# Row maxima of 16,384 rows on one core: the first load as two transfers from two queues

## The chip, the cores and the metric

The kernel runs on one core of one Trainium2 chip. The metric is the device time of one execution in microseconds (us). Lower is better.

## The reference

The input `x` has 32 x 512 rows of 1,024 float32 values, 67.11 MB in all. The output is the maximum of each row, 16,384 float32 values.

```python
def reference(x: np.ndarray) -> np.ndarray:
    return np.max(x, axis=-1).astype(np.float32)
```

## The kernel before

The 16,384 rows are dealt out to the 128 partitions of the on-chip memory, so that a partition has 128 rows (called columns of the result here). They are split into two blocks of 112 and 16 columns. Within a block, partition p holds neighbouring rows of `x`, and a load fetches n rows for each of the 128 partitions, 4 KB a row and partition. The list `BLOCKS` gives the n of each load: 2, 15, 16, 14, 11, 11, 10, 10, 8, 8, 7 for the first block and 3, 3, 3, 2, 1, 1, 1 for the second. The last two rows of each partition come as four pieces (`PIECES`), each a part of a row.

The loads go into a ring of 47 row slots in one tile named `ring`. The first four loads (2 + 15 + 16 + 14 = 47 rows) fill it exactly. Later loads reuse slots, so each must wait until the rows that lay there have been read and their transfers have landed. The function `issue()` puts each load in program order as early as the ring's list of readers lets it; all loads (line 238) and all pieces (line 243) are issued from the SP queue, one `dma_start` each. In the program's order the four loads that fill the ring stand ahead of every other step.

The work on the rows is written out by hand in `PLAN`. A step `d3` reduces all of load 3 on VectorE (DVE in the profile) with one `reduce_max`; line 78 is the helper that records every such reduction, through `in_turn`, which keeps the order of one engine's instructions. Steps `t`, `b`, `p` and `m` belong to four late loads (10, 13, 14 and 17) that are shared with other engines: TensorE transposes a part of the rows (line 160), ScalarE (ACT) copies the result out (line 166), GpSimd (POOL) reduces over the partitions (line 168), TensorE turns the maxima back (line 178), and VectorE merges. The steps `f0` to `f3` reduce the four pieces at the end. Two stores from the Activation queue (lines 265 and 267) bring the result out.

ScalarE has no work until the first copy for load 10. Its first instruction is a load of its activation table, which the compiler adds and the profile puts down to line 166.

Of the kernel before, what the change touches and what calls it, by code (L numbers as in the profile page):

```python
# [40 lines left out]
def kernel(  # L41
# [5 lines left out]
    nc = tc.nc  # L47
    P = 128
# [22 lines left out]
    def in_turn(engine, inst):  # L71
        if engine in latest:
            tc.add_manual_dep(inst.ins, latest[engine].ins.name, NOSYNC, reason="in turn")
        latest[engine] = inst
        return inst

    def maximum(out, in_):
# [8 lines left out]
        out=colno, data0=ident, data1=ident, initial=-1.0, op0=ALU.add, op1=ALU.mult))  # L86
    in_turn("DVE", nc.vector.transpose(out=rowno, in_=colno[:, :32]))  # L87
    for q in range(1, P // 32):
        part = rowno[q * 32:(q + 1) * 32, 0:1]
        in_turn("DVE", nc.vector.tensor_scalar(  # L90
            out=part, in0=part, scalar1=float(q * 32), scalar2=None, op0=ALU.add))
    identity = in_turn("DVE", nc.vector.tensor_scalar(  # L92
        out=ident, in0=colno, scalar1=rowno[:, 0:1], scalar2=None, op0=ALU.is_equal))
# [41 lines left out]
    def rows(j):  # L135
        start, n, _, _ = loads[j]
        return ring[:, I + start * D:I + (start + n) * D].rearrange("p (i d) -> p i d", d=D)
# [90 lines left out]
    issued = 0  # L228
    behind = None

    def issue():
        nonlocal issued
        while issued < len(loads):
            start, n, src, _ = loads[issued]
            if any(readers[j] and s < start + n and start < s + k
                   for j, (s, k, _, _) in enumerate(loads[:issued])):
                return
            load = nc.sync.dma_start(out=rows(issued), in_=src)  # L238
            issued += 1
        if any(readers[j] and s < at + last + 1 and at < s + k for j, (s, k, _, _) in enumerate(loads)):  # L240
            return
        while pieces:
            nc.sync.dma_start(out=pieces[0][0], in_=pieces[0][1])
            pieces.pop(0)

    for step in PLAN:
        issue()
        kind, k = step[0], int(step[1:])
        if kind in "dp":
            (direct if kind == "d" else partial)(k)  # L250
            readers[k] -= 1
        elif kind == "t":
            turn(k)
            readers[chunks[k][0]] -= 1
        elif kind == "b":
            back(k)
        elif kind == "m":
            merge(k)
        else:
            inst = maximum(*tail[k])  # L260
            if behind is None:
                behind = inst
# [34 lines left out]
```

## Time and profile before

| What | Value |
|---|---|
| time, median of 3 runs | 163.85 us (163.83 to 164.08) |
| span of the profiled execution, first to last instruction | 162.1 us |
| what the median has over that span | 1.75 us (the page gives no other time for the profiled execution) |
| VectorE busy | 135.3 us, 83% of the span |
| TensorE, ScalarE, GpSimd busy | 13.6, 6.3 and 15.9 us |
| bytes read | 67.11 MB, 414 GB/s over the span |
| queue of the loads (q1, issued from SP) | 3,168 packets, 96.8% of what 16 DMA engines can be busy in the span |
| queue of the stores (q10, issued from Activation) | 288 packets, 0.2% |

Times in the profile are counted from the first instruction. An engine's busy time leaves out the instructions that issue transfers, wait or branch. In the timeline a line gives the start, the duration, the engine, the line of the kernel, the operation with its tiles, and in brackets how long the engine was idle before it and what ended the idle time. Merged instructions have one line with their count. "SPq" is the SP engine's own instructions, here the issues of the loads.

### The profile page before, as it was taken

How to read it: one execution, taken by the hardware profiler on the slowest of the kernel's cores; microseconds unless marked ns; L12 is line 12 of the kernel's file. 1: busy time of each engine (PE TensorE's matmuls, PEld its weight loads, DVE VectorE, ACT ScalarE, POOL GpSimd, SP SyncE). 2: the span in 40 equal slices, each digit the busy share in tenths (PEclk: the TensorE clock that was granted, in tenths of full speed). 3: DMA queues.
4: the chain of work that ended last, by engine and by line, in shares of the span. 5: the costliest groups of instructions: out<-in, count | busy, mean ns of one | idle time of the engine just before them, and what ended most of it. 6: DMA issues, size and time to landing. Idle time of an engine off the chain costs nothing.

```text
span 162.1 us, 295 instructions
## 1 busy us (share of the span) xinstructions
PE 13.6 (8%) x76; PEld 11.7 (7%) x76; DVE 135.3 (83%) x33; ACT 6.3 (4%) x7; POOL 15.9 (10%) x10
## 2 busy tenths in 40 slices
PE   0000000000000000000000000000000000772942
PEld 0000000000000000000000000000000000762731
DVE  3500019998399999999999999996999999999994
ACT  3000000000000000000000000000000000241120
POOL 0000000000000000000000000000000000099791
PEclk9999999999999999999999999999999999996555
DMA  5995999599879999898999799799999989999991
GB/s 178 566 485 258 470 501 517 259 517 517 354 340 439 453 404 534 356 523 367 478 411 475 334 485 475 334 485 388 477 429 388 466 382 446 415 421 416 411 388 34
DMA packets 3456, 67.18 MB, mean 414 GB/s; under 512 B 640, under 2 KB 896, under 8 KB 1536
## 3 DMA queue, kind: packets, MB, share of 16 engines
q1 hardware_dynamic: 3168, 67.11, 96.8%
q10 hardware_dynamic: 288, 0.07, 0.2%
HBM read 67.11 MB, written 0.07 MB: 414 GB/s over the span
## 4 chain that ended last, share of the span: by engine, by line
DMA 50%; DVE 47%; SPq 1%; issue 0%; DVEq 0%
DMA ring<-in_x_dram 50%; DVE ring L78 45%; DVE joint L78 2%; SPq L238 1%; DVEq L292 0%
## 5 line engine op out<-in xcount | busy, mean ns | idle before, releaser
L78 DVE TENSOR_REDUCE ring<-ring 128x1 f32<-128x1024 f32 (+13 forms) x20 | 129.9, 6547 | 23.5 <-DMA ring<-in_x_dram 23.5
L168 POOL PARTITION_ALL_REDUCE top<-sb x6 | 15.7, 2658 | 142.6 <-ACT sb L166 142.5
L160 PE MATMUL ps<-ident,ring 128*128 128x128 f32 x38 | 9.0, 423 | 140.0 <-DMA ring<-in_x_dram 140.0
L160 PEld LDWEIGHTS ps<-ident,ring 128*128 128x128 f32 x38 | 7.6, 225 | 140.1 <-issue 140.1
L166 ACT COPY sb<-ps 128x1024 f32<-128x1024 f32 (+2 forms) x6 | 5.0, 834 | 150.5 <-PE ps L160 143.5
L78 DVE TENSOR_REDUCE joint<-ring 128x2 f32<-128x1280 f32 (+1 forms) x3 | 3.9, 1314 | 0.0
L178 PE MATMUL got<-ident,top 1*128 1x1 f32 x24 | 2.7, 228 | 3.8 <-POOL top L168 3.6
L178 PEld LDWEIGHTS got<-ident,top 1*128 1x128 f32 x24 | 2.4, 188 | 4.6 <-POOL top L168 4.6
L178 PE MATMUL joint<-ident,top 1*128 1x1 f32 x14 | 2.0, 244 | 1.9 <-POOL top L168 1.9
L178 PEld LDWEIGHTS joint<-ident,top 1*128 1x128 f32 x14 | 1.7, 210 | 2.7 <-POOL top L168 2.7
L166 ACT ACT_TABLE_LOAD x1 | 1.3, 1283 | 0.7 <-PEq L281 0.7
L83 DVE MEMSET ident<- 128x128 f32 x1 | 0.2, 165 | 0.8 <-PEq L281 0.8
L90 DVE TENSOR_SCALAR rowno<-rowno 32x1 f32<-32x1 f32 x3 | 0.4, 146 | 0.1
L85 DVE TENSOR_TENSOR_SCAN colno<-ident 128x128 f32<-128x128 f32 x1 | 0.4, 425 | 0.0
L92 DVE TENSOR_SCALAR ident<-colno,rowno 128x128 f32<-128x128 f32 x1 | 0.3, 288 | 0.0
L87 DVE STREAM_TRANSPOSE rowno<-colno 128x32 f32<-128x32 f32 x1 | 0.2, 211 | 0.0
L78 DVE TENSOR_REDUCE ring<-got 128x3 f32<-128x24 f32 x1 | 0.2, 172 | 0.0
L78 DVE TENSOR_REDUCE ring<-joint 128x5 f32<-128x20 f32 x1 | 0.2, 170 | 0.0
L281 POOL MEMSET const-float32-0.0<- 128x1 f32 x1 | 0.1, 98 | 0.2 <-issue 0.2
L281 POOL MEMSET const-bfloat16-1.0<- 128x1 bf16 x1 | 0.1, 102 | 0.0
L281 POOL MEMSET const-uint8-127<- 128x1 uint8 x1 | 0.1, 101 | 0.0
L281 POOL MEMSET const-float32-1.0<- 128x1 f32 x1 | 0.1, 98 | 0.0
(1 smaller groups left out, 0.1 us busy)
## 6 DMA issues: line engine op xcount, KB each, us to landing
ring<-in_x_dram SPq DMA_DIRECT2D x2, 5632.0 KB, 29.9
ring<-in_x_dram SPq DMA_DIRECT2D x2, 5120.0 KB, 36.8
ring<-in_x_dram SPq DMA_DIRECT2D x2, 4096.0 KB, 32.5
ring<-in_x_dram SPq DMA_DIRECT2D x1, 7680.0 KB, 22.6
ring<-in_x_dram SPq DMA_DIRECT2D x1, 7168.0 KB, 58.0
ring<-in_x_dram SPq DMA_DIRECT2D x3, 1536.0 KB, 35.7
ring<-in_x_dram SPq DMA_DIRECT2D x1, 3584.0 KB, 29.2
ring<-in_x_dram SPq DMA_DIRECT2D x2, 1024.0 KB, 17.8
```

The source lines that it names most:

```text
L78: return in_turn("DVE", nc.vector.reduce_max(out=out, in_=in_, axis=X))
L83: in_turn("DVE", nc.vector.memset(ident, 1.0))
L85: in_turn("DVE", nc.vector.tensor_tensor_scan(out=colno, data0=ident, data1=ident, initial=-1.0, op0=ALU.add, op1=ALU.mult))
L87: in_turn("DVE", nc.vector.transpose(out=rowno, in_=colno[:, :32]))
L90: in_turn("DVE", nc.vector.tensor_scalar(out=part, in0=part, scalar1=float(q * 32), scalar2=None, op0=ALU.add))
L92: identity = in_turn("DVE", nc.vector.tensor_scalar(out=ident, in0=colno, scalar1=rowno[:, 0:1], scalar2=None, op0=ALU.is_equal))
L160: in_turn("PE", nc.tensor.transpose(out=ps[:, w:w + P], in_=rows(j)[:, lead[j] + r + i, c * P:(c + 1) * P], identity=ident,))
L166: in_turn("ACT", nc.scalar.copy(out=sb[:, :W], in_=ps[:, :W]))
L168: in_turn("POOL", nc.gpsimd.partition_all_reduce(top[:, :W], sb[:, :W], P, bass_isa.ReduceOp.max))
L178: in_turn("PE", nc.tensor.transpose(out=share(j)[:, r + i, c:c + 1], in_=tops[k][0:1, w:w + P], identity=ident[0:1, 0:1],))
L238: load = nc.sync.dma_start(out=rows(issued), in_=src)
L281: nc = _bacc.Bacc("TRN2", target_bir_lowering=False, num_devices=1)
```

## The change

The first load (2 rows for each of 128 partitions, 1 MB) is issued as two transfers. The one to partitions 0 to 63 comes from the SP queue as before, the one to partitions 64 to 127 from the Activation queue. The second one is put in order with ScalarE's other work, as its first step. All other loads stay as they are.

```diff
-            load = nc.sync.dma_start(out=rows(issued), in_=src)
+            if issued:
+                nc.sync.dma_start(out=rows(issued), in_=src)
+            else:
+                nc.sync.dma_start(out=rows(issued)[:P // 2], in_=src[:P // 2])
+                in_turn("ACT", nc.scalar.dma_start(out=rows(issued)[P // 2:], in_=src[P // 2:]))
             issued += 1
```

## The prediction

> **What bounds the kernel now.** I read the page's strip of 40 slices first, then its chain, then the start of the timeline, then stretches of the span.
>
> ```profile
> DVE  3500019998399999999999999996999999999994
> DMA  5995999599879999898999799799999989999991
> q1 hardware_dynamic: 3168, 67.11, 96.8%
> DMA 50%; DVE 47%; SPq 1%; issue 0%; DVEq 0%
> ```
>
> VectorE is idle in places until about 44 us; the DMA engines are busy from the first slices to the last but one (single digits there are coarse, since a long packet is counted in one slice). The chain is half DMA and half VectorE, so I ask whether the two are late together or whether one hides the other.
>
> ```profile
> 0.72 1.28 ACT L166 ACT_TABLE_LOAD   x1 [0.72 <-PEq L281]
> 0.72 39.57 SPq L238 DMA_DIRECT2D ring<-in_x_dram  x5
> ...
> 5.65 2.29 DVE L78 TENSOR_REDUCE ring<-ring 128x2 f32<-128x2048 f32 x1 [3.14 <-DMA ring<-in_x_dram]
> 23.78 16.15 DVE L78 TENSOR_REDUCE ring<-ring 128x15 f32<-128x15360 f32 x1 [15.85 <-DMA ring<-in_x_dram]
> 43.13 17.22 DVE L78 TENSOR_REDUCE ring<-ring 128x16 f32<-128x16384 f32 x1 [3.20 <-DMA ring<-in_x_dram]
> ```
>
> The three reductions begin as loads 0, 1 and 2 land. Load 1 is 15 x 128 x 4,096 B = 7.86 MB and lands 18.13 us after load 0: 433.8 GB/s. Load 2, 8.39 MB, takes 19.35 us: 433.5 GB/s. These two equal figures are the stream's full rate.
>
> ```profile
> 43.13 66.55 DVE ring L78 x5
> 109.68 0.02 issue
> ...
> 111.01 38.94 DMA ring<-in_x_dram
> 149.95 0.02 issue
> 149.97 1.22 DVE ring L78
> ```
>
> From the chain in order of time: VectorE runs from load 2's landing to 109.68 without a break. It then waits 1.30 us for load 7 (the trace's reduction at 110.97, landed at 110.94), and from there it works to the end. All loads together, 67.11 MB at 433.5 GB/s, need 154.8 us, and the last piece lands at 159.00. So one stream of transfers runs full from about 3 us to the end, and VectorE keeps its pace. A shift of the stream at the start moves load 2's landing, VectorE's stretch behind it, the ring slots that this frees, load 7 and the tail, all by the same amount. Nothing later absorbs it, in either direction.
>
> The start is the one place where the stream is not full (DMA share and GB/s are the last two columns):
>
> ```profile
> 0.00:1.50 1.50, 0.00 (x0) 0.00 (x0) 0.65 (x4) 0.78 (x1) 0.19 (x4) 1.00 0.00 0
> 1.50:2.00 0.50, 0.00 (x0) 0.00 (x0) 0.45 (x3) 0.50 (x1) 0.00 (x0) 1.00 0.93 131
> 2.00:2.50 0.50, 0.00 (x0) 0.00 (x0) 0.45 (x3) 0.01 (x1) 0.00 (x0) 1.00 0.57 115
> 2.50:3.00 0.50, 0.00 (x0) 0.00 (x0) 0.01 (x1) 0.00 (x0) 0.00 (x0) 1.00 0.76 295
> 3.00:3.50 0.50, 0.00 (x0) 0.00 (x0) 0.00 (x0) 0.00 (x0) 0.00 (x0) 1.00 1.03 426
> ```
>
> In the packet records the first packet begins at 1.73 us, 1.01 us after the issue at 0.72, and the sixteenth chain of packets at 2.65. Packets of 8 KB take 309 ns each, those at the start up to 1,224 ns. Each DMA engine has 8 of them for load 0, and load 1's begin at 4.81 to 5.28 us.
>
> **The change part by part.** I count against the profiled span, 162.1 us, and carry the 1.75 us around it to the median of 163.85 unchanged.
>
> *The SP half.* Its issue stays at 0.72 (0.37 us long). The stream must not run dry behind it: half of load 0 is 4 packets an engine, 4 x 0.306 = 1.22 us from an effective start of about 2.4 (4.81 - 8 x 0.306), so it would be out at 3.6 at the earliest. Load 1 is issued at 1.15, and with load 0's 1.01 us to the first packet it is ready at 2.2. That cover is 1.4 us wide, so half a load on SP opens no gap: 0.
>
> *The Activation half.* One issue (0.34 to 0.38 us in the two stores from that queue) on an engine that otherwise waits until 140.95, so the engine's time is free. The page doesn't tell whether it comes ahead of the table load (issue at about 0.72) or behind it (2.00). Behind it, its first packets come at 2.00 + 1.01 = 3.0, amid load 1's. The only waiter is `d0`, which ran from 5.65 to 7.94, 15.85 us ahead of load 1; even if its packets took turns with load 1's long ones (61,440 B, 2,267 ns each), four turns of 2.6 us would bring it in by about 14 us, and `d1` waits for 23.76 in any case: 0.
>
> *The extra completion waits.* `d0` waits for two transfers in place of one, and load 4's issue on SP for one more; a wait instruction is 17 to 28 ns in the trace's SP rows. Behind `d0` on VectorE stands `d1`, behind load 4 on SP the later loads (issued from 60.38 on); all have many us to spare. One more row of completion records is 9 ns an engine. Sum 0.01 us.
>
> *The rate of the two halves.* This decides. Every load in this trace reaches all 128 partitions; none shows the rate into 64. Bound from above: the halves share the same way in and each runs at half the rate whenever it is in flight, so the 1 MB takes twice 2.42 us (1.05 MB at 433.5 GB/s): +2.42. Bound from below: they interleave perfectly, +0, and a better ramp could gain (rival two). [...] Both come near +1.2, and I take that, with 0 and 2.42 as ends.
>
> [...]
>
> Sum: 162.1 + 1.2 = 163.3 of span, 163.85 + 1.2 = 165.05 of time; 165.0 rounded.
>
> **The rivals.**
>
> *No change.* The halves interleave without loss, because each engine has packets of both queues and is kept full by load 1. For it: the stream has no gap anywhere, even between loads of very different shape, where the next load's first packet starts within 20 ns. Against it: all those are 128-partition loads on one queue. 163.85, give or take 0.2. The case where the second half is issued late, so that the two don't come at the same time, ends here too if the rate holds.
>
> *Faster, through the ramp.* With two queues each engine may get its first work sooner and have two reads in flight while the first data are late. Place: 1.73 to 2.97 us, when the last of the first packets is done. Price: from 1.73 to the effective starts of 2.36 to 2.83 (load 1's start less 8 x 0.306), 0.6 to 1.1 us are lost before; half of that back gives -0.3 to -0.55, 163.3 to 163.55. It decides once the ramp shrinks by more than what the halves lose in rate. Against it: the late starters' first packets ran at 308 to 439 ns, as if all waited for the same first data.
>
> *Full serialization.* +2.42, 166.3: the halves never use both sides, and load 1 can't fill the gap because every engine still holds packets of a half.
>
> **How the numbers follow.** A measurement of this kernel can tell about 0.2% (0.33 us) from no change; the three runs lie within 0.15%. A loss of rate of any size over 0.33 us gets 0.62, 0.42 of it for the partial loss (164.2 to 165.7) and 0.20 for one near the full 2.42. No change gets 0.17, the ramp's gain 0.21, about half of that beyond 0.45 us. The range leaves out the stronger half of the gain and a small part above the full loss: 163.4 to 166.4. The likeliest case's own range is 164.2 to 166.4.
>
> **What would show it.** Right: `d1` and `d2` start about 1.2 us later than 23.78 and 43.13, with the distance between them still 19.35; VectorE's wait for load 7 still about 1.3 us; every later landing moved alike; early stretches with a DMA share of 1 but GB/s near half of 426, or packets of 8 KB well over 309 ns. Wrong: `d1` at 23.78 or sooner with 309 ns packets (no change), the stretch from 2.0 to 3.0 us fuller than 115 and 295 GB/s (ramp), or a shift at `d1` that is gone at 110.97, which would break the step that nothing absorbs it.

## The result and the profile after

The changed kernel takes 166.30 us (median of 4 runs, 166.24 to 166.36) against 163.84 us (163.77 to 164.08) in the same comparison: slower by 2.46 us, ratio 1.0148, 95% interval 1.0136 to 1.0160. The forecast was 165.0 with a range of 163.4 to 166.4. The direction was right and the range held it, but the loss was twice the 1.2 us that I had taken.

The profiled execution has a span of 164.5 us, 2.4 us more than before. The timeline of its start (start, duration, engine):

```profile
0.72 0.54 SPq L241 DMA_DIRECT2D ring<-in_x_dram  x1
0.73 0.55 ACTq L242 DMA_DIRECT2D ring<-in_x_dram  x1
...
1.31 1.28 ACT L166 ACT_TABLE_LOAD   x1 [1.31 <-PEq L285]
1.31 41.34 SPq L239 DMA_DIRECT2D ring<-in_x_dram  x4
...
8.11 2.29 DVE L78 TENSOR_REDUCE ring<-ring 128x2 f32<-128x2048 f32 x1 [5.60 <-DMA ring<-in_x_dram]
26.14 16.15 DVE L78 TENSOR_REDUCE ring<-ring 128x15 f32<-128x15360 f32 x1 [15.75 <-DMA ring<-in_x_dram]
45.51 17.22 DVE L78 TENSOR_REDUCE ring<-ring 128x16 f32<-128x16384 f32 x1 [3.21 <-DMA ring<-in_x_dram]
```

The Activation queue's transfer is issued ahead of the table load, within 0.01 us of SP's, so the change does what it says. Loads 1 and 2 are reduced 2.36 and 2.38 us later than before, and the distance between them is 19.37 us, so the loss lies wholly ahead of load 1's landing. In the chain it stays the same to the end, as a few lines of it show:

```profile
45.51 66.55 DVE ring L78 x5
112.06 0.02 issue
...
113.40 38.93 DMA ring<-in_x_dram
152.32 0.02 issue
```

VectorE's stretch is 66.55 us long as before, and 149.95 has become 152.32. The wait for load 7 is 1.30 us as before; this is its reduction before the change and after it:

```profile
110.97 19.42 DVE L78 TENSOR_REDUCE ring<-ring 128x10 f32<-128x10240 f32 x2 [1.30 <-DMA ring<-in_x_dram]
113.35 19.41 DVE L78 TENSOR_REDUCE ring<-ring 128x10 f32<-128x10240 f32 x2 [1.30 <-DMA ring<-in_x_dram]
```

What happens at the start is seen in stretches of the span (the last two columns are the DMA engines' busy share and GB/s):

```profile
3.00:3.50 0.50, 0.00 (x0) 0.00 (x0) 0.00 (x0) 0.00 (x0) 0.00 (x0) 1.00 0.94 328
4.00:6.50 2.50, 0.00 (x0) 0.00 (x0) 0.00 (x0) 0.00 (x0) 0.00 (x0) 1.00 0.98 216
```

From 4.0 to 6.5 us the engines count as busy, 0.98, and move 216 GB/s, half of the 426 of before. The trace also has a record of every packet, with its queue, start, length and size. A record does not name its DMA engine; packets are put on one engine where the end of one meets the start of the next. In these records the 8 KB packets of the Activation queue take 613 ns (median) against 309 ns. On each of the 16 engines they come after SP's four. SP's half lands at 5.68, the other at 8.09, although both were issued at 0.72. Load 1's first packets begin at 6.51 to 7.29 us instead of 4.81 to 5.28.

### The profile page after: what moved, and what is told of

Its sections match the earlier page's. It is cut to its first block, busy times and chain, and to the rows that moved or that the text cites. A ratio compares the mean times of both kernels' runs of the same rounds, so it can differ in the third digit from the quotient of the medians.

```text
span 164.5 us, 298 instructions
## 1 busy us (share of the span) xinstructions
PE 13.3 (8%) x76; PEld 11.6 (7%) x76; DVE 135.3 (82%) x33; ACT 6.3 (4%) x7; POOL 15.9 (10%) x10
## 4 chain that ended last, share of the span: by engine, by line
DMA 50%; DVE 46%; SPq 1%; issue 0%; DVEq 0%
DMA ring<-in_x_dram 50%; DVE ring L78 44%; DVE joint L78 2%; SPq L239 1%; SPq L241 0%; DVEq L296 0%
```

## The experiments

The theory after this result (A): a transfer that goes only into partitions 0 to 63, or only into 64 to 127, runs at half the rate, and two such transfers gain nothing from being in flight together. The two halves of the partitions are called sides in some expectations. Its rivals: the second queue costs the time (B), or any transfer of 64 partitions is slow, wherever they lie (D). All ratios are against the kernel before in the same comparison, whose median was 163.82 or 163.85 us. The code cuts are against the changed kernel. Where a cut has only lines with a plus, they stand in place of the changed kernel's two transfers of the first load.

**Both halves from one queue (`e1_both_sp`).**

```diff
-                in_turn("ACT", nc.scalar.dma_start(out=rows(issued)[P // 2:], in_=src[P // 2:]))
+                nc.sync.dma_start(out=rows(issued)[P // 2:], in_=src[P // 2:])
```

> Both halves of the first load (partitions 0 to 63, then 64 to 127) are issued from SP, one after the other; nothing comes from the Activation queue at the start. [...] Theory B (a second queue costs it: the engines' switching between queues, whatever the partitions): no change, load 1's reduction near 23.8, packets of 309 ns. If the 0.31 us by which the first packet came later was due to two engines issuing at the same moment, the first packet is back at 1.73.

Measured: 166.36 us, ratio 1.0155 (1.0140 to 1.0170), as slow as the change, as A has it.

```profile
0.72 0.54 SPq L241 DMA_DIRECT2D ring<-in_x_dram  x1
...
1.32 0.57 SPq L242 DMA_DIRECT2D ring<-in_x_dram  x1
...
26.23 16.16 DVE L78 TENSOR_REDUCE ring<-ring 128x15 f32<-128x15360 f32 x1 [15.60 <-DMA ring<-in_x_dram]
```

Load 1 is reduced from 26.23 on, and the second half's packets take about 500 to 640 ns again. So the loss comes without the Activation queue, which speaks against B. The expectation on the first packet was wrong: it came at 2.06 us here too, with nothing issued beside it, and this issue too took 0.54 us against 0.37. The later start belongs to the first transfer itself, not to two engines issuing at once.

**Two queues, split by rows (`e2_rows_two_queues`).**

```diff
-                nc.sync.dma_start(out=rows(issued)[:P // 2], in_=src[:P // 2])
-                in_turn("ACT", nc.scalar.dma_start(out=rows(issued)[P // 2:], in_=src[P // 2:]))
+                nc.sync.dma_start(out=rows(issued)[:, :1], in_=src[:, :1])
+                in_turn("ACT", nc.scalar.dma_start(out=rows(issued)[:, 1:], in_=src[:, 1:]))
```

> The first load is split by rows: SP brings the first of the two rows for all 128 partitions, the Activation queue the second, at the same time, 0.5 MB each as in the change. Theory A: within 0.35 us of the kernel before (each transfer reaches both sides), at most the 0.3 us of the later first packet; packets of 4 KB near 155 ns. Theory B (the second queue costs): slower by about 2.4 us, as the change.

Measured: 163.98 us, ratio 1.0008 (0.9999 to 1.0017), no difference that can be told.

```profile
0.72 0.41 ACTq L242 DMA_DIRECT2D ring<-in_x_dram  x1
0.73 0.37 SPq L241 DMA_DIRECT2D ring<-in_x_dram  x1
```

The same two queues at the same time with the same bytes cost nothing when each transfer reaches all partitions. The packets of 4 KB took 159 ns (median), those of the two queues came interleaved (SP's from 1.74 to 4.86 us, the other's from 2.11 to 5.18), and the first came at 1.74 us as before. Together with `e1_both_sp` this rules out B.

**64 partitions across the middle (`e3_middle`).**

```diff
+                nc.sync.dma_start(out=rows(issued)[P // 4:3 * P // 4], in_=src[P // 4:3 * P // 4])
+                in_turn("ACT", nc.scalar.dma_start(out=rows(issued)[:P // 4], in_=src[:P // 4]))
+                in_turn("ACT", nc.scalar.dma_start(out=rows(issued)[3 * P // 4:], in_=src[3 * P // 4:]))
```

> SP brings partitions 32 to 95 in one transfer of 64 partitions, which lies across both halves; the Activation queue brings 0 to 31 and 96 to 127 as two. Theory A: the middle transfer runs at the full rate (packets of 8 KB near 309 ns), only the two quarters at half of it, so slower by 1.2 to 1.6 us. Theory D (any transfer of 64 partitions is at half rate, wherever they lie): the middle transfer's packets take about 610 ns and the kernel is slower by 2.4 us or more. Theory B: slower by 2.4 us or more as well, with one transfer more on the second queue, but with short packets from SP.

Measured: 165.42 us, ratio 1.0095 (1.0078 to 1.0112): +1.57, at the upper end of what A gives. The packets are mixed: of the Activation queue's last 32 (the last quarter has 32) most took about 550 to 720 ns, the middle's 310 to 750, since the three transfers were in flight together. The time speaks against D, but the packets don't separate the transfers, so a cleaner pair followed (below).

**A longer transfer in halves (`e4_load1_halves`).** Load 0 whole, load 1 in halves from the two queues.

```diff
-            if issued:
+            if issued != 1:
```

> Load 0 comes whole from SP; load 1 (7.86 MB) comes as two halves, 0 to 63 from SP and 64 to 127 from the Activation queue. So both halves are in flight together for 18 us and not for one or two. Theory A in its strict form (the halves never use both sides at once): load 1's reduction starts about 18 us later than 23.78 and the kernel takes about 182 us. Theory A in its weaker form (the second half came last in the change only because each engine had taken in the first half's four packets already; halves that are long in flight take turns): load 1 is later by something between 0 and 18 us, least if the engines fall out of step. A cost fixed per transfer: +2.4 us as in the change.

Measured: 183.37 us, ratio 1.1192 (1.1175 to 1.1209): +19.5. First the strip of GB/s in 40 slices, then the line of load 1's reduction in the timeline:

```profile
GB/s 202 273 190 217 217 217 217 217 217 462 462 275 419 434 430 582 405 318 477 477 318 477 477 434 434 434 434 434 376 462 434 376 448 405 434 434 434 395 396 77
```

```profile
43.20 16.16 DVE L78 TENSOR_REDUCE ring<-ring 128x15 f32<-128x15360 f32 x1 [30.41 <-DMA ring<-in_x_dram]
```

Each figure is a slice of 4.5 us. For six slices, while load 1 comes in, the strip shows 217 GB/s; the next four, load 2's, have 462, 462, 275 and 419. A long packet is counted in one slice, so 217 stands for one 60 KB packet from each of the 16 engines in 4.5 us. The strict form of A held: it gave about 182 us. The packet records show how the two queues shared the engines. From 13.8 us on each engine did take turns, one 60 KB packet of the one queue and one of the other, 4,631 ns each (median over load 1) against 2,267. But all 16 engines began the same turn within some 0.45 us of each other, all on 64 to 127 or all on 0 to 63. So apart from these 0.45 us only one half was being filled at a time. What two such transfers do when both halves are filled at the same moment, no run shows.

**One half alone, and the middle alone (`e5_lower_only`, `e6_middle_only`).**

```diff
+                nc.sync.dma_start(out=rows(issued)[:P // 2], in_=src[:P // 2])
+                in_turn("POOL", nc.gpsimd.memset(rows(issued)[P // 2:], 0.0))
```

In the second kernel the load has `[P // 4:3 * P // 4]` and the two outer quarters are filled with zeros.

> Of the first load only partitions 0 to 63 are fetched (0.52 MB, from SP); the other half is left out and filled with zeros by GpSimd. There is no second transfer and no second queue. Theory A (a transfer into one half of the partitions runs at half the rate): the 0.52 MB take as long as the whole 1.05 MB did at full rate, so the kernel takes about as long as before, plus up to 0.31 us if the longer issue of a 64-partition transfer (0.54 us against 0.37) delays the stream: 163.85 to 164.2. If one 64-partition transfer alone ran at the full rate and only the pair cost something: 1.21 us faster than that, 162.6 to 162.95.

> As the run with the lower half alone, but the 64 partitions fetched are 32 to 95; the rest is left out and filled with zeros. Theory A: these 64 lie on both sides, so they run at the full rate, packets near 309 ns: 162.6 to 162.95, that is 1.2 us less than with the lower half alone. Theory D (64 partitions at half rate wherever they lie): the same as the lower half alone.

Measured: 164.10 us for the lower half, ratio 1.0017 (1.0007 to 1.0027), and 163.20 us for the middle, ratio 0.9957 (0.9942 to 0.9972). Load 1's reduction in the first kernel and in the second:

```profile
23.86 16.15 DVE L78 TENSOR_REDUCE ring<-ring 128x15 f32<-128x15360 f32 x1 [15.66 <-DMA ring<-in_x_dram]
23.10 16.15 DVE L78 TENSOR_REDUCE ring<-ring 128x15 f32<-128x15360 f32 x1 [15.73 <-DMA ring<-in_x_dram]
```

The two move the same bytes with the same number of partitions, and differ by 0.90 us. The ten runs of the first lie between 163.86 and 164.63 us, all above those of the second (163.17 to 163.24). In the packet records the lower half's last packets mostly took 510 to 670 ns, the middle's 309. D has fallen. The middle was 0.25 us above the top of what I had expected. The difference is 0.9 and not 1.21, because an engine's first two packets take about as long in both kernels: taken 16 at a time in the order of their starts, the medians are 846, 366, 524 and 633 ns for the lower half, and 826, 359, 309 and 309 for the middle. Why the first two do not show the loss is open.

**Even and odd partitions (`e7_even_odd`).**

```diff
+                nc.sync.dma_start(out=rows(issued)[0::2], in_=src[0::2])
+                in_turn("ACT", nc.scalar.dma_start(out=rows(issued)[1::2], in_=src[1::2]))
```

> The first load is split into even partitions (from SP) and odd partitions (from the Activation queue), 64 each, at the same time. Both transfers reach every part of the partition range. Theory A1 (what counts is which part of the partitions a transfer spans): full rate, within 0.35 us of the kernel before. [...]

Measured: 164.20 us, ratio 1.0020 (1.0010 to 1.0029): +0.35.

```profile
0.72 0.55 SPq L241 DMA_DIRECT2D ring<-in_x_dram  x1
0.72 0.54 ACTq L242 DMA_DIRECT2D ring<-in_x_dram  x1
...
24.04 16.15 DVE L78 TENSOR_REDUCE ring<-ring 128x15 f32<-128x15360 f32 x1 [15.85 <-DMA ring<-in_x_dram]
```

As in the change there are two transfers of 64 partitions, from the same two queues, at the same moment, with the same long issues, and on each engine the Activation queue's four packets come after SP's. But the packets take 309 ns. A1 (what counts is the part of the range that a transfer spans) held, at the edge of its 0.35 us. What is left against the kernel before, 0.35 us (by the interval 0.16 to 0.48), I put down to the late start: the first packet came at 2.05 us.

**The whole first load from the other queue (`e8_whole_act`).**

```diff
+                in_turn("ACT", nc.scalar.dma_start(out=rows(issued), in_=src))
```

> The first load comes whole, 128 partitions, from the Activation queue; SP begins with load 1. Theory A: no loss of rate, so load 1 still lands near 23.7 and the kernel is within 0.35 us of the one before. The first load's packets take turns with load 1's long ones, so its reduction starts late, between 14 and 21 us, which d1 hides. Theory B (the second queue costs): slower by 2 us or more.

Measured: 163.98 us, ratio 1.0007 (0.9998 to 1.0017).

```profile
23.92 18.35 DVE L78 TENSOR_REDUCE ring<-ring 128x2 f32<-128x2048 f32 x2 [21.42 <-DMA ring<-in_x_dram]
43.13 17.22 DVE L78 TENSOR_REDUCE ring<-ring 128x16 f32<-128x16384 f32 x1 [0.86 <-DMA ring<-in_x_dram]
```

The time is as A has it. Load 0 landed later than I had said, at 23.90, because its eight packets an engine took turns with all of load 1's. VectorE then does loads 0 and 1 in one go and still waits 0.86 us for load 2. So the late load has used up all of the 15.85 us of idle time ahead of load 1 and most of the 3.20 us ahead of load 2; the 0.86 us are what is left of the cover.

**The longer transfer, even and odd (`e9_load1_even_odd`).** The edit of `e4_load1_halves` with the slices of `e7_even_odd`.

> As the run in which load 1 came as two halves (19.5 us slower), but load 1 is split into even partitions (SP) and odd partitions (Activation queue). Theory A1 (a transfer that spans all of the partition range keeps the full rate, also when two queues take turns packet by packet): packets of 60 KB back at 2,267 ns, load 1's reduction within 0.4 us of 23.78, the kernel at most 0.4 us slower. If the 19.5 us came from the turns of two long transfers on two queues and not from the halves: about 183 us again.

Measured: 163.87 us, ratio 1.0003 (0.9993 to 1.0012).

```profile
1.15 0.52 SPq L241 DMA_DIRECT2D ring<-in_x_dram  x1
...
23.70 16.16 DVE L78 TENSOR_REDUCE ring<-ring 128x15 f32<-128x15360 f32 x1 [13.67 <-DMA ring<-in_x_dram]
```

Two long transfers on two queues, taking turns packet by packet at 2,267 ns each, and nothing lost: 19.5 us of difference to `e4_load1_halves` from the choice of partitions alone. The order of the turns is the same as there, and here too all 16 engines are on the same queue's packets at a time, within 0.37 us. The issue of a 64-partition transfer is again 0.52 to 0.53 us, but here load 0 is under way and hides it.

One rival was not tried by a run. A choice of partitions is also a choice of rows of `x`: a half of the partitions reads one half of the first block's stretch of memory, so that the loss could lie where the data are read. The trace of the kernel before speaks against it. Loads 11 to 13 bring 4.72 MB into all 128 partitions out of the second block's 8.39 MB, which lie together. They come in during this stretch (the last column is GB/s):

```profile
138.88:149.95 11.07, 6.96 (x40) 6.48 (x40) 11.05 (x4) 3.04 (x3) 7.90 (x3) 0.89 1.00 423
```

At 423 GB/s, reading from one part of `x` alone does not halve the rate.

No variant was faster than the kernel before with the whole of the input fetched, so there is no better version to show.

## Why the prediction was right or wrong

**What bounds the kernel: right.** The claim that nothing absorbs a shift of the stream was the step that turned a small loss at the start into time. It held to 0.02 us: 2.36 at load 1, 2.38 at load 2 and at load 7, 2.37 at 149.95.

**The Activation half, the extra waits: right.** They cost nothing that the runs show: `e2_rows_two_queues`, with a transfer from the Activation queue and two to wait for, takes 163.98 us. The order against the table load, which I had left open, came out as issue first (0.73 against 1.31 us), so the second half did not have to wait for the 1.28 us of the table load. `e8_whole_act` shows that a late first load alone costs nothing that can be told (163.98 us), though it was later than my 14 us for the half would suggest.

**The SP half: wrong by a term.** I wrote that its issue stays at 0.72 with 0.37 us and costs 0. It took 0.54 us, and the first packet came at 2.04 us instead of 1.73. In `e7_even_odd`, which keeps this and takes the loss of rate away, the cost is 0.35 us. So a term that I had put at nothing was 0.35. (I counted 0.306 us a packet there and for the ramp, where the records have 0.309; over eight packets that is 0.02 us.) In all runs that began with a 64-partition transfer alone or with two of them, the first packet came at 2.04 to 2.10 us; with 128 partitions, or with 32 in `e3_middle`, at 1.72 to 1.75. That the longer issue is what delays the packet was not tried by itself.

**The rate of the two halves: the step that failed.** I bounded it rightly by 0 and 2.42 and took 1.2, an estimate of mine between the two. No run shows the 1.2; in its place the change against `e7_even_odd` measures 166.30 - 164.20 = 2.10 us. What I had missed is that the engines never spread over both halves. In the change each of them had the second half's four packets after the first's four, and in `e4_load1_halves`, where they did take turns, all took the same turn. That it is 2.10 and not 2.42 fits the packets: taken 16 at a time as above, the first three medians of the change's first half are 758, 338 and 422 ns (797, 309 and 309 in `e7_even_odd`), and only then do they stay above 500. Load 1's first packets, behind the halves, took 2,764 ns (median) against 2,267. Why the two queues' packets alternate in `e2_rows_two_queues` and not in the change is open. One queue or two for the halves gave 166.36 and 166.30 us, and in `e4_load1_halves` a packet took 4,793 ns behind one of the same half and 4,614 to 4,641 behind one of the other, 3% less. The trace before had no row for the value in the middle; the change came out near the upper bound.

**The rivals.** Full serialization, at 0.20, named the mechanism and the time, 166.3. The exactness is partly chance: its 2.42 stood for 2.10 of lost rate and 0.35 of a late start that it didn't have. The ramp's gain did not show: with the halves the stretch from 2 to 3 us moved 197 GB/s against 205. Even `e2_rows_two_queues`, where both queues feed the engines nearly from the first moment at full rate, gained nothing that can be told.

## What to carry to other kernels

A transfer into partitions 0 to 63, or 64 to 127, runs at about half the rate here (8 KB packets of about 620 and 613 ns in the change, against 309), and a second one into the other half at the same time does not make it good (217 GB/s in `e4_load1_halves` against 433.5 before). Split a load so that each part spans the whole range of partitions (by rows, 163.98 us, or by even and odd partitions, 164.20 us, against 166.30 for the halves), or leave it whole (163.84 us). Where a stream of transfers is full from its start to the end, expect any loss at the start to count in full, as the 2.36 us at load 1 did here. Where the rows give only two bounds for a term, carry them as a range and do not take the middle as its value.

## What was not expected of the hardware

- 64 partitions as such are not slow: 32 to 95, the even ones and the odd ones all came to 309 ns for 8 KB a packet (`e6_middle_only`, `e7_even_odd`), where 0 to 63 came to about 620 (the fourth 16 of the change).
- Engines that take turns between two queues stayed in step with each other over the whole of load 1, more than 30 us (`e4_load1_halves`); the packets there took 4,631 ns (median), 2% more than twice 2,267.
- The issue of a 64-partition transfer took 0.52 to 0.59 us, that of a 128-partition one 0.37 to 0.41 as the first of its queue; a stream that begins with one starts about 0.3 us later.
